# Wider products in a two-block transformer kernel: 512-column feed-forward products, 33-column slot factors, 512-column memory slabs

## The chip, the core and the metric

The kernel runs on one core of a Trainium2 chip. The metric is the device time of one execution in microseconds, lower is better. The engines are called as in the profile: PE (TensorE matmul), PEld (TensorE weight load, which overlaps PE), DVE (VectorE), ACT (ScalarE), POOL (GpSimd) and SP (SyncE, whose queue issues the loads).

## The reference, cut to what matters

256 tokens of width 1024 pass through two blocks in float32. The first block is an attention mixer and a mixture of 32 experts (each token goes to 2 of them), the second has two layers, each a mixer, a cross-attention into 256 memory tokens and a gated feed-forward with a causal convolution of width 3 over the tokens.

```python
# experts, after the choice of 2 of 32 per token (weight = group share * softmax of the two)
ys = (silu(xb @ w_g[e]) * (xb @ w_u[e])) @ w_d[e]
out = zeros(T, D).at[slot_tok].add(ys * slot_w)

def mem_attention(h, mem_n, w_q, w_kv, q_gain, k_gain, w_o):
    kv = (mem_n @ w_kv).reshape(B, M, 2, X_HEADS, X_HEAD_DIM)
    k, v = rmsnorm(kv[:, :, 0], k_gain), kv[:, :, 1]
    ...

def conv_ffn(h, w_up, w_conv, w_down):          # w_up 1024 x 5632, w_down 2816 x 1024
    u = causal_dwconv(h @ w_up, w_conv)
    gate, val = split(u, 2)
    return (silu(gate) * val) @ w_down
```

## The kernel before, in words

**Products.** Every large product is made of split numbers: a weight slab `w` (128 x 2048, 1 MB) is loaded by SP's queue, ACT copies it to the rounded `h` in two halves of 1024 columns, and DVE makes the remainder `l` = `w` - `h`, also in halves (`slab`, line 554). The activations are split in the same way into `xh` and `xl` (`parts`, `norm_parts`, `xtiles`, line 593). A product is then three matmuls, `h`·`xh`, `l`·`xh` and `h`·`xl` (`mm3`, line 575). `fm` (line 678) makes one PSUM bank of two 128-row halves by 256 tokens from 8 pieces of the depth, so 48 matmuls of 256 columns. `tm` with `by_token_products` and `by_token_wide` (lines 693 to 709) makes the transposed form, tokens by 256 or by 512 columns.

**Feed-forward** (`ffn`, line 1567). 22 pairs, each 128 gate and 128 value columns. Per pair: one `fm` (48 matmuls), a DVE product with the reciprocal root mean square that also evicts the bank (`fu<-fm,rbc`), four DVE convolution steps (`fc<-fu,partile,fc`), Silu on ACT, gate times value on DVE, and the split of the result into `fa`. After every second pair comes `down`, 24 to 48 matmuls of 512 or 256 columns (`dn`) that add to four banks which are held throughout. In the second layer these four banks first receive the residual `x`, transposed by 16 products with the identity (lines 1572 to 1576), and the epilogue copies them out, two by ACT and two by DVE.

**Experts** (`moe`, line 1061). Four gathers of 8 experts each (`gather`, line 1112): DVE makes a 0/1 selection `st` and two scaled copies of it, `rt` (times the token's norm factor `rtm`) and `ct` (times its weight); PE gathers the tokens (`ga`) and takes 8 one-column products of `rt` and `ct` (`rs`), which give each slot's norm and weight. Expert weights go straight from the load into the products (`gu<-w,xs`, `by`), without a split, and take any spare buffer. Steps of the memory part (`memory`, line 1335: per layer one `prepare`, four `values` of 256 columns by `by_token_products` and four `keys`) are filled in: `MEM_EARLY` ahead of the first gather, `MEM_EVERY` per group.

**Order.** The helper records every operation (all at line 471 of the profile), and `plan` (line 292) lays them out per engine by a list schedule with costs from `price`; loads stay in recorded order unless a due time moves them (`touch`, line 261 in the part on first uses, sets how a tile's first load is ranked). PSUM has 3 banks of tag `g` (`fm`, `tm`, `ga`), 2 of `a`, 2 of `b`, 1 of `m` (`bank`, line 486). `w`, `h` and `l` have 3 buffers each.

Of the kernel before, what the change touches and what calls it, by code (L numbers as in the profile page):

```python
# [25 lines left out]
NPAIR = 22  # L26
WARM = 44
# [6 lines left out]
MEM_EARLY = 2  # L34
FILL = 300
LATEG = 1
MEM_EVERY = (2, 2, 2, 2, 2, 2, 1, 0)
# [16 lines left out]
for _name, _width in (("ident", 128), ("cmask", 128), ("smask", 128), ("ulow", 128), ("ntri", 128),  # L54
                      ("bd64", 128), ("dist", 256), ("cm", 32), ("sm", 32), ("cb", 16), ("sb", 16),
                      ("slot", 32)):
    CST[_name] = (_off, _off + _width)
    _off += _width
# [104 lines left out]
class Recorder:  # L163
# [310 lines left out]
class Net:  # L474
# [118 lines left out]
    def xtiles(self):  # L593
        return [self.rec.tile([128, KC, T], F32R, n, n, 2) for n in ("xh", "xl")]
# [72 lines left out]
    def norm_parts(self, src, gain, stats=True):  # L667

        acc = None
        xh, xl = self.xtiles()  # L670
# [5 lines left out]
        return (xh, xl), acc  # L676

    def fm(self, w, x, kcs=None, cols=0, name="fm", tag="g"):

        (h, l), _ = w  # L680
        xh, xl = x
# [10 lines left out]

    def tm(self, b, w, x, kcs, t, cols, first=True, last=True):

        (h, l), _ = w
        xh, xl = x
# [275 lines left out]
    def route(self, rtm):  # L972
# [16 lines left out]
        def small(name, *s):  # L989
            if name in ("wt", "place", "wlate"):  # L990
                return self.small(name, 2, *s, bufs=1)
# [26 lines left out]
        sel, wt = small("sel", 4, 8), small("wt", 4, 8)  # L1018
# [3 lines left out]
        sel, wtf = (q.rearrange("p t g e -> p t (g e)") for q in (sel, wt))  # L1022
# [36 lines left out]
        return wtf, place, wlate, flag  # L1059

    def moe(self, steps, early, every):
        nc, a, x = self.rec, self.a, self.x

        hh, hl = (t.rearrange("p (t q) n -> p t (q n)", t=2) for t in self.xtiles())
# [9 lines left out]
        wt, place, wlate, flag = self.route(rtm)  # L1074
# [5 lines left out]
        xs, rest = self.gather(0, hh, hl, place, wt, rtm)  # L1080
        banks = [self.bank("a", "gu")]
        self.gate_up(0, range(KC), xs, banks[0])
        for g in range(8):
# [17 lines left out]
            if g % 2 == 0 and g < 6:  # L1101
                ahead, later = self.gather(g // 2 + 1, hh, hl, place, wt, rtm)
# [9 lines left out]
    def gather(self, p, hh, hl, place, wt, rtm):  # L1112
# [3 lines left out]
        ct, rt = (self.temp("b", n, [128, 2, 8, SLOTS]) for n in ("ct", "rt"))  # L1116
        for t in range(2):
# [3 lines left out]
            nc.vector.tensor_scalar(rt[:, t], st[:, t], rtm[:, t:t + 1], None, ALU.mult)  # L1121
            nc.vector.tensor_tensor(ct[:, t], st[:, t], pe(wt), ALU.mult)
        stv, ctv, rtv = (v.rearrange("p t e s -> p t (e s)") for v in (st, ct, rt))
        xs = self.big("xs", [128, KC, 256])
        for i in range(4):
# [6 lines left out]
            for j in range(2):  # L1132
# [4 lines left out]
                else:  # L1137
                    nc.vector.tensor_scalar(xs[:, c, :], b[:, 256 * j:256 * j + 256], gc, None, ALU.mult)
        b = self.bank("m", "rs")
# [6 lines left out]
        nc.vector.tensor_copy(rw, b[:, :4])  # L1146

        b = self.bank("m", "sb")
        for i in range(2):
            for t in range(2):  # L1150
                o = 256 * i + 128 * t
                nc.tensor.transpose(b[:, o:o + 128], stv[:, t, 128 * i:128 * i + 128].step("bitcast", F32), self.ident)
# [121 lines left out]
    def two_norms(self):  # L1274
# [7 lines left out]
        xh, xl = self.xtiles()  # L1282
# [52 lines left out]
    def memory(self):  # L1335
# [5 lines left out]
        def prepare(l):  # L1341
# [4 lines left out]
            xh, xl = self.xtiles()  # L1346
# [17 lines left out]
        def keys(l, s):  # L1364
            b = self.fm(self.slab(a[f"w_xkv{l}"][s], 256), state["x"], tag="b" if l and s > 1 else "g")
# [3 lines left out]
        def values(l, s):  # L1369
            bs = self.by_token_products(self.slab(a[f"w_xkv{l}"][4 + s], 256), state["x"])  # L1370
            for t in range(2):
                nc.scalar.activation(self.mem_v[l][:, t, 256 * s:256 * s + 256], bs[t][:, :256], AF.Copy,
# [3 lines left out]
        for l in range(2):  # L1376
            steps.append(lambda l=l: prepare(l))
            steps += [lambda l=l, s=s: values(l, s) for s in range(4)]
# [188 lines left out]
    def ffn(self, l, out=None):  # L1567
# [12 lines left out]
        def down(i):  # L1580
# [10 lines left out]
            else:  # L1591
                for t in range(2):
                    s = slice(128 * t, 128 * t + 128)
                    for n in range(2):
                        m = slice(512 * n, 512 * n + 512)
                        self.mm3([(acs[2 * t + n], part(0, k, s), part(1, k, s), h[:, k, m], lo[:, k, m], False,
                                   i == ndown - 1 and k == 1) for k in range(2)])

        for i in range(NPAIR):
            p = "ab"[i % 2]  # L1600
            b = self.fm(self.slab(a[f"w_up{l}"][i], 256), x)
# [46 lines left out]
def layouts(i):  # L1648
# [41 lines left out]
    for l in range(2):  # L1690
        o[f"w_xq{l}"] = slabs(f["x_w_q_2"][l], 8, 256)
        o[f"w_xkv{l}"] = slabs(f["x_w_kv_2"][l], 8, 256)
# [39 lines left out]
def shape_constants():  # L1732
# [15 lines left out]
    for cn, sn, half in (("cm", "sm", 16), ("cb", "sb", 8)):  # L1748
# [3 lines left out]
        for n, fn in ((cn, np.cos), (sn, np.sin)):  # L1752
            put(n, fn(ang.astype(np.float64)).reshape(2, 128, half).transpose(1, 0, 2))
    put("slot", np.broadcast_to(np.arange(SLOTS) - 999.0, (128, SLOTS)))
# [17 lines left out]
```

## Time and profile before

| | before |
|---|---|
| median of 3 runs (lowest to highest) | 1273.33 us (1271.55 to 1277.99) |
| profiled execution: its own time / span | 1273.8 / 1272.0 us |
| mean granted clock over the span | 0.982 of full speed |
| PE, DVE, ACT busy | 1219.8, 862.5, 647.9 us |
| DMA | 273.5 MB, mean 215 GB/s |

An execution's own time is 1.8 us more than its span. A chain piece is a stretch in which the named engine was the one that the end waited for. Names are out<-in with buffer numbers left out. Where PE runs back to back, the time of a matmul is the step from one to the next, since each one's listed duration overlaps its neighbours.

### The profile page before, as it was taken

Reading aid. Unit: us, or ns where it says so; the run is one execution under the profiler, and the core shown is the slowest. Engines: PE = TensorE matmul, PEld = TensorE weight load, DVE = VectorE, ACT = ScalarE, POOL = GpSimd, SP = SyncE. Lnnn points to the kernel's source line nnn. Section 1 sums busy time; section 2 is a strip of 40 time slices with the busy share of each in tenths; the row PEclk is TensorE's granted clock in tenths of the full one; section 3 lists DMA queues with packets and bytes.
Section 4 is the critical chain, followed back from the end, with each engine's and each line's share of the span. In section 5 each row is a group of like instructions: output and inputs, shape, how many; then the busy total and the mean of one; then the engine's idle time right before and its main releaser. Section 6 shows DMA issues by size and latency. Waiting matters only on the chain.

```text
span 1272.0 us, 22373 instructions
## 1 busy us (share of the span) xinstructions
PE 1219.8 (96%) x9175; PEld 1074.6 (84%) x9175; DVE 862.5 (68%) x1546; ACT 647.9 (51%) x1095; POOL 7.9 (1%) x70
## 2 busy tenths in 40 slices
PE   9999999997889978998999999999999999999998
PEld 9988999664555644897999999999989999999997
DVE  7667677424462345997777977777755587877775
ACT  7655554223332235554555655455767655555543
POOL 0000000000000000000000000000000000000000
PEclk9999999998899999998999999999999999999999
DMA  7633665899999997542541555454433252555551
GB/s 274 237 103 130 217 247 199 340 405 417 382 398 419 415 381 282 199 153 80 181 151 67 210 195 182 177 199 168 172 125 135 103 178 97 185 199 171 187 176 64
DMA packets 40140, 273.51 MB, mean 215 GB/s; under 512 B 4576, under 2 KB 4576, under 8 KB 8032
## 3 DMA queue, kind: packets, MB, share of 16 engines
q1 hardware_dynamic: 40032, 272.03, 57.5%
q8 instruction: 73, 1.20, 0.4%
q14 instruction: 35, 0.29, 0.1%
HBM read 270.96 MB, written 1.05 MB: 214 GB/s over the span
## 4 chain that ended last, share of the span: by engine, by line
PE 68%; DVE 5%; ACT 3%; issue 1%; DVEq 0%; ACTq 0%
PE fm L471 41%; PE dn L471 10%; PE tw L471 3%; PE gu L471 2%; PE tm L471 2%; PE oz L471 2%; DVE l L471 1%; PE mo L471 1%; PE by L471 1%; PE ms L471 1%; PE hn L471 1%; PE bo L471 1%; ACT h L471 1%; DVE x L471 1%; PE co L471 1%
## 5 line engine op out<-in xcount | busy, mean ns | idle before, releaser
L471 PE MATMUL fm<-xh,h 128*128 128x256 f32 x1824 | 527.3, 290 | 5.1 <-ACT h L471 2.9
L471 PE MATMUL fm<-xh,l 128*128 128x256 f32 x1824 | 519.8, 285 | 6.2 <-DVE l L471 6.2
L471 PE MATMUL fm<-xl,h 128*128 128x256 f32 x1824 | 519.5, 285 | 0.0
L471 DVE TENSOR_TENSOR l<-w,h 128x1024 fp32r<-128x1024 f32 (+2 forms) x328 | 383.6, 1192 | 60.8 <-ACT h L471 59.3
L471 ACT ACTIVATE h<-w 128x1024 fp32r<-128x1024 f32 (+2 forms) x328 | 325.9, 1028 | 170.7 <-issue 87.3
L471 PEld LDWEIGHTS fm<-xh,h 128*128 128x128 f32 x1824 | 351.4, 193 | 16.6 <-ACT h L471 5.8
L471 PEld LDWEIGHTS fm<-xh,l 128*128 128x128 f32 x1824 | 351.6, 193 | 9.0 <-DVE l L471 8.6
L471 PEld LDWEIGHTS fm<-xl,h 128*128 128x128 f32 x1824 | 351.7, 193 | 6.5 <-issue 5.1
L471 DVE SCALAR_TENSOR_TENSOR fc<-fu,partile,fc 128x256 f32<-128x256 f32 x176 | 73.5, 480 | 1.3 <-ACT fc L471 1.3
L471 PE MATMUL gu<-w,xs 128*32 128x512 f32 x512 | 68.7, 644 | 0.1
L471 PE MATMUL dn<-fa,h 128*128 128x256 f32 x352 | 64.2, 282 | 1.1 <-ACT fa L471 0.6
L471 PE MATMUL tm<-l,xh 128*128 128x256 f32 (+2 forms) x204 | 59.9, 294 | 2.7 <-DVE l L471 2.7
L471 PE MATMUL tm<-h,xh 128*128 128x256 f32 (+2 forms) x204 | 61.1, 300 | 0.8 <-DVE x L471 0.6
L471 PE MATMUL tm<-h,xl 128*128 128x256 f32 (+2 forms) x204 | 59.7, 294 | 0.0
L471 PE MATMUL dn<-h,fa 128*128 128x512 f32 x176 | 57.0, 396 | 0.0
L471 DVE TENSOR_TENSOR fu<-fm,rbc 128x512 f32<-128x512 f32 x44 | 30.3, 688 | 37.9 <-PE fm L471 37.6
L471 PEld LDWEIGHTS dn<-fa,h 128*128 128x128 f32 x352 | 54.4, 189 | 1.6 <-ACT fa L471 0.8
L471 DVE SCALAR_TENSOR_TENSOR yl<-by,rw,yh 128x512 fp32r<-128x512 f32 x16 | 12.0, 749 | 55.7 <-ACT yh L471 55.7
L471 PE MATMUL dn<-fa,l 128*128 128x256 f32 x176 | 49.6, 282 | 0.0
L471 ACT ACTIVATE fc<-fc 128x256 f32<-128x256 f32 x44 | 18.4, 419 | 56.2 <-DVE fc L471 56.2
L471 PEld LDWEIGHTS tm<-h,xh 128*128 128x128 f32 x204 | 39.7, 195 | 5.4 <-issue 2.5
L471 PEld LDWEIGHTS tm<-l,xh 128*128 128x128 f32 x204 | 39.9, 196 | 3.5 <-DVE l L471 3.1
(285 smaller groups left out, 1545.5 us busy)
## 6 DMA issues: line engine op xcount, KB each, us to landing
w<-w_gu SPq DMA_DIRECT2D x64, 1024.0 KB, 10.8
w<-w_up SPq DMA_DIRECT2D x44, 1024.0 KB, 4.9
w<-w_dn SPq DMA_DIRECT2D x32, 1024.0 KB, 12.2
w<-w_down SPq DMA_DIRECT2D x22, 1024.0 KB, 4.9
w<-w_xkv SPq DMA_DIRECT2D x16, 1024.0 KB, 8.8
w<-w_in_d SPq DMA_DIRECT2D x8, 1024.0 KB, 4.9
w<-w_xq SPq DMA_DIRECT2D x8, 1024.0 KB, 4.9
w<-w_xo SPq DMA_DIRECT2D x8, 1024.0 KB, 4.9
```

The costliest lines, as they stand in the source:

```text
L471: self.last[engine.engine] = getattr(engine, method)(*map(r, a), **{n: r(v) for n, v in k.items()})
```

## The change

1. **Feed-forward in 512 columns.** For pairs 3 to 19 of the 22, in both layers, `fm_wide` takes the place of `fm`. The tile `xx` now holds `xh` and `xl` side by side, so per half and piece of the depth one matmul `h`·[`xh`|`xl`] of 512 columns and one `l`·`xh` of 256 stand where three of 256 stood. Each half has a bank of its own, whose two column halves must be added: ACT copies the first 256 columns to `fu`, DVE adds the second 256, and then the product with `rbc` runs from SBUF.
2. **Second layer's residual.** The 16 identity products at the start are gone; at pair 5, 16 transposes go through the one `m` bank into `xt` (4 ACT copies), and the epilogue is four DVE additions.
3. **Gather.** `rt` and `ct` are gone. `rs` is four products per gather of the selection with `factors` (33 columns: norm factor and 32 weights), followed by a copy, a mask product with the constant `own` and a short reduction.
4. **Memory values.** Two half-input slabs of 512 columns per step by `by_token_wide`, two steps per layer instead of four; `MEM_EARLY` 1, `MEM_EVERY` (1,2,2,2,1,1,1,0).
5. **One tile for both activation parts**, and in the rank of a tile's first use the time that the planner allows a load to land (`lag`) is now taken off too.

```diff
-            op.preds.setdefault(t.first.idx, -t.first.cost)
+            op.preds.setdefault(t.first.idx, -t.first.cost - t.first.lag)
...
     def xtiles(self):
-        return [self.rec.tile([128, KC, T], F32R, n, n, 2) for n in ("xh", "xl")]
+        both = self.rec.tile([128, 2, KC, T], F32R, "xx", "xx", 2)
+        return both[:, 0], both[:, 1], both
...
+    def fm_wide(self, w, x):
+        (h, l), _ = w
+        xh, _, both = x
+        bs = []
+        for j in range(2):
+            b = self.bank("g", "fw")
+            s = slice(128 * j, 128 * j + 128)
+            for k in range(KC):
+                self.rec.record("tensor", [
+                    ("matmul", (b[:, :512].rearrange("p (a b) -> p a b", a=2), h[:, k, s], both[:, :, k, :]),
+                     dict(start=k == 0, stop=False, skip_group_check=True)),
+                    ("matmul", (b[:, :T], l[:, k, s], xh[:, k, :]),
+                     dict(start=False, stop=k == KC - 1, skip_group_check=True))])
+            bs.append(b)
+        return bs
...
-            nc.vector.tensor_scalar(rt[:, t], st[:, t], rtm[:, t:t + 1], None, ALU.mult)
-            nc.vector.tensor_tensor(ct[:, t], st[:, t], pe(wt), ALU.mult)
...
-        for n, v in enumerate((rtv, ctv)):
-            for i in range(2):
-                for t in range(2):
-                    self.mm(b[:, 2 * n + i:2 * n + i + 1], v[:, t, 128 * i:128 * i + 128], self.kone,
-                            t == 0, t == 1)
+        for i in range(2):
+            for t in range(2):
+                self.mm(b[:, 64 * i:64 * i + 33], one(t, i), factors[:, t, :], t == 0, t == 1)
...
         def values(l, s):
-            bs = self.by_token_products(self.slab(a[f"w_xkv{l}"][4 + s], 256), state["x"])
+            bs = self.by_token_wide([self.slab(w, 512) for w in a[f"w_xv{l}"][2 * s:2 * s + 2]], state["x"])
...
-        if out is not None:
-            for c in range(KC):
-                for t in range(2):
-                    self.mm(acs[2 * t + c // 4][:, 128 * (c % 4):128 * (c % 4) + 128],
-                            self.x[:, c, 128 * t:128 * t + 128], self.ident, c % 4 == 0, False)
...
-            nc.vector.tensor_tensor(u[:, :, 2:], self.two(b), self.rep(rbc), ALU.mult)
+            if NARROW <= i < NPAIR - 2:
+                for n, b in enumerate(self.fm_wide(slab, x)):
+                    nc.scalar.activation(u[:, n, 2:], b[:, :T], AF.Copy)
+                    nc.vector.tensor_tensor(u[:, n, 2:], u[:, n, 2:], b[:, T:], ALU.add)
+                nc.vector.tensor_tensor(u[:, :, 2:], u[:, :, 2:], self.rep(rbc), ALU.mult)
...
+            if i == 5 and out is not None:
+                xt = self.big("xt", [128, 2, D])
+                for t in range(2):
+                    for n in range(2):
+                        b = self.bank("m", "xt")
+                        for j in range(4):
+                            nc.tensor.transpose(b[:, 128 * j:128 * j + 128],
+                                                self.x[:, 4 * n + j, 128 * t:128 * t + 128], self.ident)
+                        nc.scalar.activation(xt[:, t, 512 * n:512 * n + 512], b, AF.Copy)
...
-                if i % 2:
-                    nc.vector.tensor_copy(o, acs[i])
-                else:
-                    nc.scalar.activation(o, acs[i], AF.Copy)
+                nc.vector.tensor_tensor(o, acs[i], xt[:, t, 512 * n:512 * n + 512], ALU.add)
```

**How it moves the instructions.** First DVE in the first layer's feed-forward, pairs 10 and 11 (`fu` the up-projection, `fc` its convolution, `fa` the split result, `l` the slabs' remainders); before:

```order
L471 TENSOR_TENSOR fu<-fm,rbc 128x2x256
L471 TENSOR_TENSOR l<-w,h 128x1024
L471 SCALAR_TENSOR_TENSOR fc<-fu,partile,fc 128x256 x4
L471 TENSOR_TENSOR l<-w,h 128x1024
L471 TENSOR_TENSOR fc<-fc 128x256
L471 TENSOR_TENSOR fa<-fc,fa 128x256
L471 TENSOR_TENSOR fu<-fm,rbc 128x2x256
```

After, the same pairs, from the addition for pair 10's second half:

```order
L472 TENSOR_TENSOR fu<-fu,fw 128x256
L472 TENSOR_TENSOR l<-w,h 128x1024
L472 TENSOR_TENSOR fu<-fu,rbc 128x2x256
L472 TENSOR_TENSOR fu<-fu,fw 128x256
L472 SCALAR_TENSOR_TENSOR fc<-fu,partile,fc 128x256 x4
L472 TENSOR_TENSOR l<-w,h 128x1024
L472 TENSOR_TENSOR fu<-fu,fw 128x256
L472 TENSOR_TENSOR fc<-fc 128x256
L472 TENSOR_TENSOR fu<-fu,rbc 128x2x256
```

The addition for pair 11's first half now stands ahead of pair 10's convolution, so the convolution is behind a wait for PE's next half.

Next PE at the first gather (`ga` the gathered tokens, `gu` the first expert group); before:

```order
L471 MATMUL ga<-st,xl 128x256
L471 MATMUL rs<-order,rt 128x1 x4
L471 MATMUL rs<-order,ct 128x1 x4
L471 MATMUL gu<-w,xs 32x512 x4
L471 MATMUL sb<-csttile,st 128x128 x4
```

After:

```order
L472 MATMUL ga<-st,xx 128x256 x2
L472 MATMUL rs<-factors,st 128x33
L472 MATMUL ga<-st,xx 128x256 x28
L472 MATMUL rs<-factors,st 128x33 x3
L472 MATMUL gu<-w,xs 32x512 x4
L472 MATMUL sb<-csttile,st 128x128 x4
```

Half as many `rs` products stand between the gather and the first expert product, and no `ct` or `rt` is waited for.

Last, SP at the head of the program (three slabs of `w_in_a` in quarters, and the quarters of `x`); before:

```order
2 L471 DMA x_87<-x 128x512
3 L471 DMA w_100<-w_in_a 128x512
4 L471 DMA w_113<-w_in_a 128x512
5 L471 DMA w_126<-w_in_a 128x512
6 L471 DMA x_87<-x 128x512
7 L471 DMA w_100<-w_in_a 128x512
8 L471 DMA x_87<-x 128x512
```

After:

```order
2 L472 DMA x_87<-x 128x512
3 L472 DMA w_100<-w_in_a 128x512
4 L472 DMA x_87<-x 128x512
5 L472 DMA w_100<-w_in_a 128x512
6 L472 DMA x_87<-x 128x512
7 L472 DMA w_100<-w_in_a 128x512
8 L472 DMA x_87<-x 128x512
9 L472 DMA w_100<-w_in_a 128x512
10 L472 DMA w_153<-w_in_a 128x512 x4
11 L472 DMA w_168<-w_in_a 128x512 x4
```

The first quarters of the second and third slab have moved from ahead of the second quarter of `x` to behind the whole of `x` and the first slab.

## Rows read from the trace of the kernel before

**Rows 1.** The page: busy time of each engine, and the chain's shares by engine and line.

```profile
PE 1219.8 (96%) x9175; PEld 1074.6 (84%) x9175; DVE 862.5 (68%) x1546; ACT 647.9 (51%) x1095; POOL 7.9 (1%) x70
...
PE 68%; DVE 5%; ACT 3%; issue 1%; DVEq 0%; ACTq 0%
PE fm L471 41%; PE dn L471 10%; PE tw L471 3%; PE gu L471 2%; PE tm L471 2%; PE oz L471 2%; DVE l L471 1%; PE mo L471 1%; PE by L471 1%; PE ms L471 1%; PE hn L471 1%; PE bo L471 1%; ACT h L471 1%; DVE x L471 1%; PE co L471 1%
```

**Rows 2.** The chain's pieces in order of time: start, length, engine, product, instructions.

```profile
514.47 7.04 PE tw L471 x31
...
729.06 11.52 PE fm L471 x96
740.57 5.76 PE dn L471 x48
...
1075.82 3.57 PE dn L471 x32
...
1108.47 11.51 PE fm L471 x96
1119.98 5.61 PE dn L471 x24
```

**Rows 3.** Stretch, length, then busy: two feed-forwards, experts; last granted clock, DMA share, GB/s.

```profile
729.06:867.24 138.18, 138.18 (x1154) 138.18 (x1154) 105.25 (x161) 73.24 (x113) 1.35 (x13) 1.00 0.53 185
1108.47:1245.43 136.96, 136.96 (x963) 128.19 (x962) 105.37 (x161) 73.09 (x113) 1.34 (x13) 1.00 0.53 184
225.00:500.00 275.00, 236.60 (x1738) 147.57 (x1737) 113.02 (x211) 86.02 (x126) 0.00 (x0) 0.94 0.98 398
```

**Rows 4.** DVE's longest wait between 1108 and 1245 us: total, times, longest.

```profile
DVE fu L471 <- PE fm L471: 16.1, 8, 2.1
```

**Rows 5.** Groups of instructions with shapes kept apart: busy, mean ns of one, idle before.

```profile
L471 DVE TENSOR_TENSOR l<-w,h 128x1024 fp32r<-128x1024 f32 x306 | 367.3, 1222 | 55.4 <-ACT h L471 53.9
...
L471 DVE SCALAR_TENSOR_TENSOR fc<-fu,partile,fc 128x256 f32<-128x256 f32 x176 | 73.5, 480 | 1.3 <-ACT fc L471 1.3
...
L471 DVE TENSOR_TENSOR xl<-bo,xh 128x256 fp32r<-128x256 f32 x16 | 6.7, 420 | 8.8 <-ACT xh L471 8.8
L471 ACT ACTIVATE xh<-bo 128x256 fp32r<-128x256 f32 x16 | 6.1, 383 | 10.0 <-PE bo L471 9.9
...
L471 DVE TENSOR_TENSOR ct<-st,wt 128x256 f32<-128x256 f32 x8 | 3.3, 418 | 0.0
```

**Rows 6.** PE in order of time, end of the first attention and start of the experts.

```profile
210.73 1.03 PE L471 MATMUL xt<-csttile,x 128*128 128x128 f32 x8
211.70 0.62 PE L471 MATMUL rt<-x,wr 128*36 128x256 f32 x2
...
233.17 0.95 PE L471 MATMUL rs<-order,rt 128*128 128x1 f32 x8
233.98 1.03 PE L471 MATMUL rs<-order,ct 128*128 128x1 f32 x8
234.94 1.07 PE L471 MATMUL gu<-w,xs 128*32 128x512 f32 x8
```

**Rows 7.** What SP's queue waited for between 225 and 500 us.

```profile
SPq L471 <- PE gu L471: 88.0, 45, 8.1
SPq L471 <- DVE l L471: 62.9, 10, 8.9
```

**Rows 8.** PE, then DVE, at the head, in order of time.

```profile
5.56 0.39 PE L471 MATMUL fm<-xh,h 128*128 128x256 f32 x1
...
25.00 0.28 PE L471 MATMUL fm<-xh,l 128*128 128x256 f32 x1
...
9.16 0.87 DVE L471 SCALAR_TENSOR_TENSOR xl<-x,partile,xh 128x256 fp32r<-128x256 f32 x2
10.02 0.69 DVE L471 TENSOR_TENSOR l<-w,h 128x512 fp32r<-128x512 f32 x1
10.63 0.69 DVE L471 TENSOR_TENSOR acc<-acc,sq 128x512 f32<-128x512 f32 x1
```

More of the change, by code (lines that the diff above doesn't have):

```diff
@@ L669, in norm_parts @@
         acc = None
-        xh, xl = self.xtiles()
+        xh, xl, both = self.xtiles()
         for i in range(4):
@@ L1058, in route @@
         nc.vector.tensor_copy(flag[0:1, :], b[0:1, 0:1])
-        return wtf, place, wlate, flag
+        return factors, place, wlate, flag
     def moe(self, steps, early, every):
         nc, a, x = self.rec, self.a, self.x
-        hh, hl = (t.rearrange("p (t q) n -> p t (q n)", t=2) for t in self.xtiles())
+        hh, hl = (t.rearrange("p (t q) n -> p t (q n)", t=2) for t in self.xtiles()[:2])
         for q in range(2):
@@ L1073, in moe @@
         rtm = self.rstd_by_token(self.sumsq(x))
-        wt, place, wlate, flag = self.route(rtm)
+        factors, place, wlate, flag = self.route(rtm)
         nc.bias = -FILL
@@ L1079, in moe @@
         self.next = []
-        xs, rest = self.gather(0, hh, hl, place, wt, rtm)
+        xs, rest = self.gather(0, hh, hl, place, factors)
         banks = [self.bank("a", "gu")]
@@ L1101, in moe @@
             if g % 2 == 0 and g < 6:
-                ahead, later = self.gather(g // 2 + 1, hh, hl, place, wt, rtm)
+                ahead, later = self.gather(g // 2 + 1, hh, hl, place, factors)
             if q:
@@ L1110, in moe, with gather @@
                 steps.pop(0)()
-    def gather(self, p, hh, hl, place, wt, rtm):
+    def gather(self, p, hh, hl, place, factors):
         nc, slot = self.rec, self.c("slot")
         st = self.temp("a", "st", [128, 2, 8, SLOTS], F32R)
-        ct, rt = (self.temp("b", n, [128, 2, 8, SLOTS]) for n in ("ct", "rt"))
         for t in range(2):
@@ L1138, in gather @@
                     nc.vector.tensor_scalar(xs[:, c, :], b[:, 256 * j:256 * j + 256], gc, None, ALU.mult)
+        one = lambda t, i: stv[:, t, 128 * i:128 * i + 128].step("bitcast", F32)
         b = self.bank("m", "rs")
-        for n, v in enumerate((rtv, ctv)):
-            for i in range(2):
-                for t in range(2):
-                    self.mm(b[:, 2 * n + i:2 * n + i + 1], v[:, t, 128 * i:128 * i + 128], self.kone,
-                            t == 0, t == 1)
-        rw = self.small("rw", 4)
-        nc.vector.tensor_copy(rw, b[:, :4])
+        for i in range(2):
+            for t in range(2):
+                self.mm(b[:, 64 * i:64 * i + 33], one(t, i), factors[:, t, :], t == 0, t == 1)
+        bv = b[:, :128].rearrange("p (i n) -> p i n", i=2)
+        rw = self.small("rw", 4)
+        own = self.small("own", 2, 8, bufs=1)
+        nc.vector.tensor_copy(rw[:, 0:2], bv[:, :, 0])
+        nc.vector.tensor_tensor(own, bv[:, :, 1 + 8 * p:9 + 8 * p],
+                                self.c("own").rearrange("p (i e) -> p i e", i=2), ALU.mult)
+        nc.vector.tensor_reduce(rw[:, 2:4], own, axis=AX.X, op=ALU.add)
         b = self.bank("m", "sb")
@@ L1151, in gather @@
                 o = 256 * i + 128 * t
-                nc.tensor.transpose(b[:, o:o + 128], stv[:, t, 128 * i:128 * i + 128].step("bitcast", F32), self.ident)
+                nc.tensor.transpose(b[:, o:o + 128], one(t, i), self.ident)
         sb = self.small("sb", 2, T, dt=F32R)
@@ L1364, in keys @@
         def keys(l, s):
-            b = self.fm(self.slab(a[f"w_xkv{l}"][s], 256), state["x"], tag="b" if l and s > 1 else "g")
+            b = self.fm(self.slab(a[f"w_xk{l}"][s], 256), state["x"], tag="b" if l and s > 1 else "g")
             self.head_norm("ab"[s % 2], b, self.k256, True, state["r"], self.mem_k[l][:, s],
@@ L1377, in memory @@
             steps.append(lambda l=l: prepare(l))
-            steps += [lambda l=l, s=s: values(l, s) for s in range(4)]
+            steps += [lambda l=l, s=s: values(l, s) for s in range(2)]
             steps += [lambda l=l, s=s: keys(l, s) for s in range(4)]
@@ L1595, in down @@
                         m = slice(512 * n, 512 * n + 512)
-                        self.mm3([(acs[2 * t + n], part(0, k, s), part(1, k, s), h[:, k, m], lo[:, k, m], False,
-                                   i == ndown - 1 and k == 1) for k in range(2)])
+                        self.mm3([(acs[2 * t + n], part(0, k, s), part(1, k, s), h[:, k, m], lo[:, k, m],
+                                   i == 0 and k == 0, i == ndown - 1 and k == 1) for k in range(2)])
         for i in range(NPAIR):
             p = "ab"[i % 2]
-            b = self.fm(self.slab(a[f"w_up{l}"][i], 256), x)
+            slab = self.slab(a[f"w_up{l}"][i], 256)
             u = self.temp(p, "fu", [128, 2, T + 2])
             nc.gpsimd.memset(u[:, :, 0:2], 0.0)
-            nc.vector.tensor_tensor(u[:, :, 2:], self.two(b), self.rep(rbc), ALU.mult)
+            if NARROW <= i < NPAIR - 2:
[3 more added lines that the diff above has]
+                nc.vector.tensor_tensor(u[:, :, 2:], u[:, :, 2:], self.rep(rbc), ALU.mult)
+            else:
+                nc.vector.tensor_tensor(u[:, :, 2:], self.two(self.fm(slab, x)), self.rep(rbc), ALU.mult)
             cs = self.temp(p, "fc", [128, 2, T])
@@ L1691, in layouts @@
         o[f"w_xq{l}"] = slabs(f["x_w_q_2"][l], 8, 256)
-        o[f"w_xkv{l}"] = slabs(f["x_w_kv_2"][l], 8, 256)
+        o[f"w_xk{l}"] = slabs(f["x_w_kv_2"][l][:, :1024], 8, 256)
+        o[f"w_xv{l}"] = halves(f["x_w_kv_2"][l][:, 1024:])
         o[f"w_xo{l}"] = slabs(f["x_w_out_2"][l], 8, 256)
@@ L1753, in shape_constants @@
             put(n, fn(ang.astype(np.float64)).reshape(2, 128, half).transpose(1, 0, 2))
+    put("own", np.arange(8)[None, None, :] == 4 * np.arange(2)[None, :, None] + r[:, :, None] // 32)
     put("slot", np.broadcast_to(np.arange(SLOTS) - 999.0, (128, SLOTS)))
```

32 lines of the change are left out of this document (19 added, 13 removed).

## The prediction, made before the changed kernel was run

> **What bounds the kernel now.** I read the busy totals first, then the chain of waits, then the stretches. PE is busy for 1219.8 of 1272.0 us, and the chain goes through PE for 68% of the span, through DVE for 5% and ACT for 3%; 41% of the span is the feed-forward's up-projection alone [rows 1]. So what shortens PE's stream in the feed-forwards shortens the kernel, as long as nothing else ends later. The chain's pieces give the pace: 96 matmuls of 256 columns in 11.52 us, 0.120 us each; 31 matmuls of 512 columns in 7.04 us, 0.227 each; in the down-projection of layer 1, 24 of 512 columns in 5.61 us, 0.234 each [rows 2]. In both feed-forwards PE fills eight rounds (two pairs and one down-projection each) without a gap, 136.96 us or 17.12 per round in layer 1, while DVE works 105.37 and ACT 73.09 [rows 3]: DVE has 13.17 us of work per round and idles 3.95, ACT has 9.14. DVE's largest wait there is for PE's finished bank [rows 4]. The experts are another regime: between 225 and 500 us PE is busy for 236.60 of 275 us, but the DMA engines for 98% of it, at 398 GB/s [rows 3], and SP's queue waits for `gu` products to give buffers back, 88.0 us in 45 waits [rows 7]. There transfers set the end, and PE time saved is worth nothing until the transfers end earlier.
>
> The sum stands against the profiled execution's own 1273.8 us, 0.5 us above the median of 1273.33. A measurement of this kernel can tell about 0.5%, 6.4 us: faster is below 1266.96, slower above 1279.7.
>
> **Term 1, the merged products.** 17 pairs in 2 layers, 8 pieces of the depth and 2 halves make 544 places where two matmuls of 256 columns become one of 512. Two cost 0.240. The one costs 0.2271 by the memory rows or 0.2338 by the down-projection [rows 2], the nearest rows there are; both multiply the same number format with a weight load per matmul. Saved: 544 × 0.0129 = 7.0 or 544 × 0.0062 = 3.4 us. I take the middle, 0.2305, since the down-projection shares the stage and the memory rows the form: **−5.2**.
>
> **Term 2, layer 1's opening.** The identity products go: 32 instructions, 3.57 us [rows 2]. The 16 transposes that come instead step at 0.121 us by the eight that took from 210.73 to 211.70 [rows 6]: 1.94 us. Net −1.6. They use the only `m` bank in four groups, so each group may wait for ACT to empty it (up to 1.65 us, an estimate: a 512-column ACT copy behind one 1.05 us half of `h`); products of the next pair stand between the groups and cover most of that. Bounds −1.6 and 0; I take **−1.1**.
>
> **Term 3, the first gather.** Here PE waits for no transfer: `rs` takes from 233.17 to 234.94, 1.77 us for 16 instructions [rows 6]. Half of them remain, 33 columns instead of one: −0.9. The memory steps filled in ahead of the gather change from 96 matmuls of 256 columns (11.5 us) to 48 of 512 (11.06): −0.45. Together **−1.35**. The scaled copies (`ct` takes 0.418 us each [rows 5], `rt` less) lay behind those fillers, so their removal adds nothing on the path; the tiny mask and sum stand beside the `sb` transposes.
>
> **Term 4, the other experts.** The bytes are the same: 16 memory slabs, eight of them in another form. Two slabs must now be there before a `values` step ends, and both hold a `w` buffer, which queues SP's next expert loads behind DVE's `l` (already 62.9 us in 10 waits [rows 7]); against that, two steps fewer per layer and no `rt`/`ct` let buffers go sooner. The transfers leave 2% of 275 us open, 5.5 us [rows 3]; that is the most that tighter queueing could give back, and I put as much on the other side. I take **0**, bounds −5 and +5.
>
> **Term 5, the head.** Loads of the second and third slab move behind `x`. Before, the first 144 products took from 5.56 to 25.12 us [rows 8], 2.3 more than 144 × 0.12. After, in the first four quarters only one slab is there: 12 products, 1.44 us per quarter, against DVE's 0.87 + 0.69 + 0.69 = 2.25 [rows 8] for the quarter of `xl`, `l` and the squares. Three such gaps of 0.81 are 2.4. With the queue of three more loads behind, **+0.4**; bounds −1 and +1.5.
>
> **Term 6, the new evictions.** Per round four ACT copies of 256 columns from PSUM (0.383 each by `xh<-bo`) and four DVE additions (0.420 each by `xl<-bo,xh`) are added [rows 5]; the `rbc` product stays. DVE: 13.17 + 1.68 = 14.85; ACT: 9.14 + 1.53 = 10.7. PE's new round is 2 × 16 × (0.2305 + 0.120) + 5.6 = 16.8. Both fit, so **0**; what hides them is PE, and the cover on DVE is 2.0 us per round where it was 3.95. With three `g` banks a half's bank is wanted again two halves later, 5.6 us; its drain is an ACT copy and an addition, behind at most one `l` half of 1.22 and four convolution steps of 0.48 each [rows 5]: 0.38 + 1.22 + 1.92 + 0.42, some 4 us. If that cover went, each round would be late by what is missing, times 17. The end gains nothing: the four additions replace copies behind the same last products.
>
> The sum: −5.2 − 1.1 − 1.35 + 0 + 0.4 + 0 = −7.25, so **1266.5 us**.
>
> **Rivals.** *The wide product gains nothing (chance 0.13).* If the pace goes by columns, a merged product costs as much as its two parts and term 1 is 0: 1273.8 − 1.1 − 1.35 + 0.4 = 1271.8. For it: the two 512-column rows differ by 0.007, half of the saving, and the one of this very stage is the dearer. Against it: even that one saves 0.006. The Trainium skill ("TensorE: Matmul & The Clock Gate", section Back-to-back issue gap) gives an isolated gap of N/2.4 + 2.5 ns, by which one product in place of two saves only 2.5 ns, 544 × 2.5 = 1.4 us, an estimate, and the kernel would come out at 1270.4. The trace speaks against it: 0.120 at 256 columns, where that rule has 0.109, leaves 13 ns per instruction over the columns.
>
> *DVE becomes the feed-forward's bound (chance 0.13, slower).* The place is DVE's queue in the rounds: the addition for the next pair's first half now stands ahead of this pair's convolution, so the convolution, Silu, `fa` and the down-projection behind them wait for PE's next half. It decides as soon as DVE's waits per round exceed the 2.0 us left. Today they are 3.95, nearly all for PE or ACT. If three quarters remain, 2.96, the round is 14.85 + 2.96 = 17.8, 0.7 more than 17.12; 17 rounds add 11 us in place of term 1: 1273.8 + 11 − 2.05 = 1282.8. Against it: waits for PE shrink by themselves when DVE is fuller, since work that waits for nothing (six halves of `l`) fills them. The Trainium skill ("Perfetto Trace Analysis", section Identifying Performance Opportunities) reads the same gap repeated on the saturated engine as a sign of too few buffers; three banks for twice as many evictions would be such a place, and PE showed no such gap in these rounds before.
>
> *The experts' transfers lose (chance 0.13):* term 4 at +5, 1271.5. For it: two slabs hold buffers at once; against it: SP's queue already runs ahead until it waits for a buffer. *They gain (chance 0.16):* term 4 at −5, 1261.5.
>
> **How the numbers follow.** The forecast has the remaining chance, 0.45. Its own range by the bounds of terms 1 to 3 and 5 is 1262.9 (−7.0 − 1.6 − 1.35 − 1) to 1270.6 (−3.4 − 1.35 + 1.5); 0.25 of it lies below 1266.96 and 0.20 above. With the gaining transfers (0.16) faster has 0.41; the first and third rival with 0.20 give 0.46 for no change; the DVE rival gives 0.13 for slower. The range goes from 1258.5 (term 4 at −5 and term 1 at its better bound give 1259.8, and the head may gain) to 1276 (the transfers' loss with the worse bounds of terms 1, 2 and 5: 1275.6); outside are the DVE rival and a small rest.
>
> **What would show it.** Term 1: the wide matmuls step at 0.227 to 0.234 and a round takes 16.8 us with no PE gap. Term 2: no `dn` piece before the first `fm` of layer 1, and at most short gaps among the transposes. Term 3: the first `gu` starts about 1.35 us earlier, near 233.6. Term 4: the stretch from the first to the last expert product keeps its length and its DMA share. Term 5: 144 head products end near 25.5. The prediction is wrong if PE shows gaps behind `fa` or a `g` bank in the rounds (DVE's bound), or if the experts' stretch changes by more than 5 us.

## The result and the profile after

The changed kernel takes 1262.17 us (median of 5 runs, 1260.68 to 1265.47) against 1273.33: a ratio of 0.9901 with a 95% interval from 0.9875 to 0.9927. That is faster by 11.2 us, more than the 6.4 that the prediction set as its bound. The forecast was 1266.5, and 1258.5 to 1276 its range; faster had the chance 0.41 there and no change 0.46. The profiled execution took 1262.97 us; the page says:

```profile
span 1261.2 us, 20928 instructions
...
PE 1208.7 (96%) x8391; PEld 1026.1 (81%) x8391; DVE 878.7 (70%) x1609; ACT 671.4 (53%) x1157; POOL 7.6 (1%) x70
...
PE 66%; DVE 4%; DMA 3%; ACT 2%; issue 1%; ACTq 0%; DVEq 0%
PE fm L472 26%; PE fw L472 15%; PE dn L472 10%; PE tw L472 4%; DMA w<-w_dn 3%; PE gu L472 2%; PE oz L472 2%; PE mo L472 1%; PE ms L472 1%; PE by L472 1%; DVE l L472 1%; PE hn L472 1%; PE bo L472 1%; PE co L472 1%; ACT h L472 1%; DVE rsq_t L472 1%
```

Against [rows 1], PE lost 11.1 us of work and still bounds the kernel; DVE gained 16.2 and ACT 23.5 us. DMA now has a share of the chain, most of it two loads of an expert's weights (`w_dn`) for which the end waited: the experts' part is told below.

I cut both traces at the same places of the program and compared the lengths of the pieces, each from the first instruction of one product to that of the next one named:

| piece of the program | before | after | difference |
|---|---|---|---|
| start to the transposed norm `bt` | 25.21 | 25.86 | +0.65 |
| `bt` to the first expert product `gu` | 209.73 | 208.64 | -1.09 |
| experts: first `gu` to the 31 `tw` after them | 279.18 | 278.75 | -0.43 |
| even mixer, to the last `mo` of layer 0 | 169.43 | 168.29 | -1.14 |
| feed-forward of layer 0, to the first `oz` | 225.89 | 221.45 | -4.44 |
| odd mixer and cross-attention, to the last `mo` | 150.10 | 150.19 | +0.09 |
| feed-forward of layer 1 and output | 212.46 | 207.97 | -4.49 |
| span | 1272.00 | 1261.15 | -10.85 |

Each column is one execution. The experts' piece scatters most: in the five kernels below that have the changed kernel's experts (experiments 1, 2, 4, 7 and 8) it takes 276.35 to 278.74 us, so its -0.43 could as well be -2.8.

**The feed-forwards.** The chain's pieces (start, length, engine, product, instructions) show the rounds that answer to [rows 2]:

```profile
726.87 11.09 PE fw L472 x64
737.97 5.70 PE dn L472 x48
743.66 11.11 PE fw L472 x64
754.77 5.64 PE dn L472 x48
...
1092.81 5.60 PE dn L472 x24
1098.42 11.10 PE fw L472 x64
...
1133.81 11.30 PE fw L472 x64
1145.11 5.60 PE dn L472 x24
```

Two pairs take 11.10 us where they took 11.52: 32 merged products and 32 single ones, 0.347 per couple. With 0.120 for the single one, the 512-column product costs 0.227, the better of the two bounds. PE has no gap, and the stretch that answers to the first in [rows 3] (columns as there) says how far DVE and ACT were from the bound:

```profile
720.00:860.85 140.85, 140.85 (x953) 130.04 (x953) 120.27 (x204) 88.65 (x152) 1.44 (x14) 1.00 0.55 190
```

Per round of 16.74 us DVE works 14.3 (120.27 / 140.85 × 16.74) and ACT 10.5; the prediction had 14.85 and 10.7.

**Layer 1's opening.** PE, in order of time, at the transposes that took the place of the identity products (start, duration):

```profile
1114.95 0.60 PE L472 MATMUL xt<-csttile,x 128*128 128x128 f32 x4
1115.30 0.48 PE L472 MATMUL fw<-xx,h 128*128 128x512 f32 x1
...
1116.80 0.66 PE L472 MATMUL xt<-csttile,x 128*128 128x128 f32 x4
1117.21 0.47 PE L472 MATMUL fw<-xx,h 128*128 128x512 f32 x1
```

Each group of four takes 0.35 to 0.41 us, and eight products run until the next group; no group waits for ACT to empty the one bank.

**The experts' first products.** What answers to [rows 6]:

```profile
233.82 0.75 PE L472 MATMUL rs<-factors,st 128*128 128x33 f32 x6
234.50 1.07 PE L472 MATMUL gu<-w,xs 128*32 128x512 f32 x8
```

The `rs` products between the gather and the first expert product shrank from 1.77 to 0.68 us. The start of `gu` itself moved only from 234.94 to 234.50, since the head came later.

**One difference that is not the change's.** The even mixer's 1.14 us lie after a stretch in which PE had little to do. The program is the same there, but TensorE came back from the lower to the higher of its two clock levels at another moment. From both traces, the stretch after PE's restart; the third number from the end is the granted clock. Before (restart at 590.36):

```profile
592.00:596.00 4.00, 4.00 (x22) 4.00 (x21) 2.10 (x8) 0.42 (x1) 0.00 (x0) 0.53 0.00 0
```

After (restart at 589.30):

```profile
590.00:594.00 4.00, 4.00 (x26) 4.00 (x26) 3.01 (x10) 1.01 (x5) 0.00 (x0) 0.68 0.01 2
```

The kernels of experiments 9 and 11 run the same instructions in the same order up to the end of this piece, and it takes 169.51 and 168.53 us in them. So such a microsecond comes and goes without an edit, and it belongs to no term.

### The profile page after: what moved, and what is told of

It reads as the page before. It is cut to its first block, busy times and chain, and to the rows that moved or that the text cites. A ratio compares the mean times of both kernels' runs of the same rounds, so it can differ in the third digit from the quotient of the medians.

```text
span 1261.2 us, 20928 instructions
## 1 busy us (share of the span) xinstructions
PE 1208.7 (96%) x8391; PEld 1026.1 (81%) x8391; DVE 878.7 (70%) x1609; ACT 671.4 (53%) x1157; POOL 7.6 (1%) x70
## 4 chain that ended last, share of the span: by engine, by line
PE 66%; DVE 4%; DMA 3%; ACT 2%; issue 1%; ACTq 0%; DVEq 0%
PE fm L472 26%; PE fw L472 15%; PE dn L472 10%; PE tw L472 4%; DMA w<-w_dn 3%; PE gu L472 2%; PE oz L472 2%; PE mo L472 1%; PE ms L472 1%; PE by L472 1%; DVE l L472 1%; PE hn L472 1%; PE bo L472 1%; PE co L472 1%; ACT h L472 1%; DVE rsq_t L472 1%
## 5 line engine op out<-in xcount | busy, mean ns | idle before, releaser
L472 PE MATMUL fm<-xx,h 128*128 128x256 f32 x2560 | 485.4, 290 | 5.2 <-DVE cu L472 2.2
L472 PEld LDWEIGHTS fm<-xx,h 128*128 128x128 f32 x2560 | 406.5, 194 | 20.2 <-issue 11.9
L472 PE MATMUL fm<-xx,l 128*128 128x256 f32 x1280 | 367.3, 287 | 8.5 <-DVE l L472 8.4
L472 PEld LDWEIGHTS fm<-xx,l 128*128 128x128 f32 x1280 | 247.8, 194 | 12.7 <-DVE l L472 10.7
L472 PE MATMUL fw<-xx,h 128*128 128x512 f32 x544 | 190.8, 394 | 0.0
L472 PE MATMUL fw<-xx,l 128*128 128x256 f32 x544 | 152.3, 280 | 0.0
L472 PEld LDWEIGHTS fw<-xx,h 128*128 128x128 f32 x544 | 101.9, 187 | 22.7
L472 PEld LDWEIGHTS fw<-xx,l 128*128 128x128 f32 x544 | 102.7, 189 | 0.3
L472 PE MATMUL tw<-h,xx 128*128 128x512 f32 x288 | 95.9, 399 | 0.2 <-DVE x L472 0.2
L472 PE MATMUL tw<-l,xx 128*128 128x512 f32 x144 | 57.2, 397 | 2.1 <-DVE l L472 2.1
```

What stands on the lines that cost most here:

```text
L472: self.last[engine.engine] = getattr(engine, method)(*map(r, a), **{n: r(v) for n, v in k.items()})
```

## The experiments

All kernels ran beside the kernel before on the same chip; ratios are to it. Pieces are those of the table, from one execution each.

**1. The products split again.** Two matmuls of 256 columns for each of 512, everything else as in the changed kernel.

```diff
-("matmul", (b[:, :512]..., h[:, k, s], both[:, :, k, :]), ...),
+("matmul", (b[:, :T], h[:, k, s], both[:, 0, k, :]), ...),
+("matmul", (b[:, T:], h[:, k, s], both[:, 1, k, :]), ...),
```

> The changed kernel with each 512-column product of the feed-forward written as two of 256 again; banks per half, copies and additions stay. Theory (a matmul costs its columns plus some 13 ns, so merging is what saves): 32 merged pairs of matmuls, 11.10 to 11.30 us now, go back to 11.5 per two pairs, a round to about 17.2 in both layers, and the time to about 1262.2 + 7 = 1269. Rival (the saving comes from the bank per half and the shorter eviction, not from merging): rounds stay at 16.7 to 16.8 and the time within 1.5 of 1262.

Measured: 1268.83 us, ratio 0.9958 (0.9943 to 0.9973), 6.7 above the changed kernel by the medians. Its chain in layer 0:

```profile
726.40 11.51 PE fw L472 x96
737.91 5.63 PE dn L472 x48
```

The up-projection is back at 11.51, so merging is what saves: 0.41 us per 32 merges, 13 ns each in these rounds. The two feed-forward pieces take 224.71 and 210.54 us, 5.83 more than in the changed kernel, which is 10.7 ns for each of the 544 merges. The down-projection of layer 0 stays at 5.63 where it was 5.76 [rows 2]; that small gain is not the merging's.

**2. The old ranking of loads.**

```diff
-op.preds.setdefault(t.first.idx, -t.first.cost - t.first.lag)
+op.preds.setdefault(t.first.idx, -t.first.cost)
```

> The changed kernel with the old ranking of first uses (no lag), so the first quarters of the second and third slab load ahead of the second quarter of x again. Theory (the head's new load order lost 0.65 us): first product near 5.6, the 48 products after the head's norm start 0.65 earlier (25.4 against 26.07) and the time is 1261.5. Rival (the rank also sets the order of later loads, above all among the experts): the head is the same or better, and the experts' stretch changes by more than 1 us in either direction.

Measured: 1261.33 us, ratio 0.9909 (0.9876 to 0.9943). `bt` came at 24.67 us against 25.86, but over all profiles of this study it lies between 24.67 and 27.80 with the old ranking and between 25.61 and 27.05 with the new one, medians 25.7 and 25.9. The head's 0.65 us are within what the first loads scatter, and this run does not settle the term.

**3. Memory values in 256 columns again,** with `MEM_EARLY` 2 and the old steps.

```diff
-bs = self.by_token_wide([self.slab(w, 512) for w in a[f"w_xv{l}"][2 * s:2 * s + 2]], state["x"])
+bs = self.by_token_products(self.slab(a[f"w_xv{l}"][s], 256), state["x"])
```

> The changed kernel with memory values in slabs of 256 columns, four steps per layer, filled in as before (2 early, then 2,2,2,2,2,2,1,0); the gather and the feed-forward stay changed. Theory (the two-slab step holds the loads up: between 355 and 375 us the DMA moved 311 and 198 GB/s, some 6 us lost, while the new gather saves elsewhere): that hole goes, the experts' stretch from the first expert product to the 31 products at 513 us shrinks from 278.75 to about 274, the time to about 1258. Rival one (bytes set the stretch, holes only move): 278 to 280 and 1262 to 1263. Rival two (the wide values saved in other places what the hole cost): 283 or more and 1266.

Measured: 1258.49 us, ratio 0.9872 (0.984 to 0.9904), and the experts' piece of the table takes 273.09 us instead of 278.75. The changed kernel lost it in one place. Two stretches of its trace (columns as in [rows 3], the last two are the DMA share and GB/s):

```profile
355.00:365.00 10.00, 9.20 (x68) 4.56 (x67) 6.63 (x16) 6.57 (x13) 0.00 (x0) 1.00 0.80 311
365.00:375.00 10.00, 8.73 (x58) 2.68 (x56) 3.02 (x6) 0.73 (x2) 0.00 (x0) 0.83 0.58 198
```

SP's queue, in order of time, shows why: behind 358.21 nothing is issued until both slabs of layer 1's first values find buffers at 370.07.

```profile
358.21 0.99 SPq L472 DMA_DIRECT2D w<-w_dn  x2
370.07 1.59 SPq L472 DMA_DIRECT2D w<-w_xv  x2
```

With single slabs the queue waits there too, but only until 359.78, and the same stretches read:

```profile
355.00:365.00 10.00, 8.57 (x67) 3.76 (x66) 7.46 (x17) 6.57 (x13) 0.00 (x0) 1.00 0.96 388
365.00:375.00 10.00, 8.43 (x65) 3.51 (x65) 3.56 (x7) 3.05 (x4) 0.00 (x0) 1.00 1.02 425
```

So the experts' part was 6.1 us shorter than before once the slabs were as before: something else in the change gives 6 us there. The kernels of experiments 5, 9 and 11 run the same experts' code as this one and take 272.64, 272.55 and 271.78 us.

**4. The old opening of layer 1's feed-forward,** identity products and copies.

```diff
+if out is not None:
+    for c in range(KC):
+        for t in range(2):
+            self.mm(acs[2 * t + c // 4][:, ...], self.x[:, c, 128 * t:128 * t + 128], self.ident, c % 4 == 0, False)
...
-if i == 5 and out is not None:
...
```

> The changed kernel with the 16 identity products ahead of the second feed-forward of layer 1 and the old epilogue of copies. Theory (PE's stream there is the bound, and the 16 transposes cost 1.8 us where the products cost 3.57): 1.8 us more, 1264. Rival (the products ran while PE would have waited for the norm anyway, so nothing is gained by moving them): the first product of the up-projection starts no later than now relative to the mixer's end, and the time stays at 1262.

Measured: 1263.13 us, ratio 0.9913 (0.9883 to 0.9942), too near to tell by the time alone. The trace tells it: from the last `mo` to the end 209.72 us against 207.97, 1.75 more.

**5. The new gather alone** in the kernel before; it also has the one tile for both activation parts, which the new code brings. Of the change's diff only the parts on `gather`, `route` (`factors`), `own` and `xtiles` stay:

```diff
-for n, v in enumerate((rtv, ctv)):
...
+self.mm(b[:, 64 * i:64 * i + 33], one(t, i), factors[:, t, :], t == 0, t == 1)
```

> The kernel before with the new gather alone (33-column products, no scaled copies): no wide products in the feed-forward, 256-column memory slabs, old opening and epilogue, old ranking of loads. With 256-column slabs the experts' stretch took 273.1 us, against 279.2 before, so something in the gather must have given 6. Theory (the scaled copies and the products that waited for them held the loads: SP's queue waited 6.5 us for one copy before): first expert product 0.9 earlier, the stretch behind it about 273 to 274, the time 1273.5 - 0.9 - 5.5 = 1267. Rival (the order that the planner chose for the other changed parts gave it, and the gather gives only its own products): the stretch stays at 278 to 280 and the time is 1272.5.

Measured: 1266.07 us, ratio 0.9935 (0.9912 to 0.9959), and 272.64 us for the experts' piece. The gather gives 6.5 us in this piece, and the traces show where. PE at the second gather, before (in brackets the idle time and its releaser):

```profile
246.49 1.90 PE L471 MATMUL by<-w,act 128*32 128x512 f32 x16
250.34 0.35 PE L471 MATMUL rs<-order,rt 128*128 128x1 f32 x2 [1.94 <-DVE rt L471]
...
252.03 1.84 PE L471 MATMUL rs<-order,ct 128*128 128x1 f32 x8
...
254.10 0.63 PE L471 MATMUL co<-sb,yh 128*128 128x256 f32 x2
```

And with the new gather:

```profile
246.19 1.90 PE L472 MATMUL by<-w,act 128*32 128x512 f32 x16
248.02 1.08 PE L472 MATMUL rs<-factors,st 128*128 128x33 f32 x8
...
250.51 0.40 PE L472 MATMUL co<-sb,yh 128*128 128x256 f32 x2
```

Before, PE stood for 1.94 us behind a scaled copy that DVE had not made yet, and then TensorE ran at its lower level (what brought it is not shown; see experiment 6): the granted clock was 0.80 of full from 245 to 255 us against 1.00, and the 16 `rs` products took 3.4 us where the first gather's took 1.77. The first expert output `co` came 19.2 us after the first `gu` instead of 15.9. The rest was lost at the last gather: between the 65th and the 81st `co` matmul before took 37.3 us and this kernel 33.9. PE waited for no scaled copy there; 14 of the 16 `rs` products stood in one block ahead of `sb`:

```profile
406.40 0.83 PE L471 MATMUL rs<-order,rt 128*128 128x1 f32 x6
407.10 1.03 PE L471 MATMUL rs<-order,ct 128*128 128x1 f32 x8
```

Each expert product that comes late gives its buffer back late [rows 7], and the loads queue behind it: the `w_dn` pair after the second gather is issued at 265.54 us before and at 261.46 here. The down-projections of layer 0 take 5.63 us in this kernel too, so their small gain is neither the merging's nor the wide slabs'. The one tile `xx` is what the feed-forward here shares with experiment 1, but no run has that tile alone, so the cause is open.

**6. The same with the scaled copies made, but read by nobody.**

```diff
+nc.vector.tensor_scalar(rt[:, t], st[:, t], factors[:, t, 0:1], None, ALU.mult)
+nc.vector.tensor_tensor(ct[:, t], st[:, t], pe(factors[:, :, 1:33]), ALU.mult)
```

> The gather_only kernel with the two scaled copies of the selection made again on DVE in every gather, but read by nobody. Theory (what held the experts was PE, which stood in order behind products that waited for the copies): with no product behind them the copies cost next to nothing, the first expert output (co) comes 15.9 us after the first expert product as without them, the stretch stays at 272.6 to 274, the time at 1266 to 1267. Rival (DVE's time and the two buffers they take cost it, or their place in DVE's order): co comes at 18 to 19 us, the stretch is 276 to 279 and the time 1270 to 1272.

Measured: 1269.78 us, ratio 0.9964 (0.9949 to 0.9979), between the two. Its profiled execution was 8.8 us above its median, so I took one more.

> The same kernel with unread scaled copies once more, for a profile near its median of 1269.8 (the profiled execution of the first was 8.8 us above it). It is 3.7 above the kernel without the copies, half of what the whole gather gave. Theory one (the wait in PE's order at the second gather was worth the first 3.2 us, and copies anywhere in DVE's queue cost the rest later): first expert output at 15.4 to 15.9 us after the first expert product, and the 3 to 4 us are lost at a later gather, behind the copies in DVE's queue. Theory two (the planner's order with the copies differs elsewhere): the loss stands at a place with no copy near it.

Measured: 1269.83 us. The first `co` comes 15.4 us after the first `gu`, so it was PE's products behind the copies that cost 3 us up to there. The ninth is 1.6 us later than in experiment 5, but there TensorE ran at its lower level again, this time without a wait for a copy:

```profile
245.00:255.00 10.00, 8.35 (x58) 4.61 (x57) 6.82 (x15) 2.58 (x3) 0.00 (x0) 0.85 1.01 425
```

That delay is gone by the 33rd `co`, where this kernel is 0.1 us ahead of experiment 5. By the 81st it is 1.9 late, where the kernel before is 6.5 late. Another 2.7 us are lost between the 89th and 97th, with no copy near. It takes 25.5 us for these eight steps and experiment 5 takes 22.9. But experiments 3 and 11, which run the same experts' code as experiment 5 and make no copy, take 25.5 too, so that loss says nothing of the copies or of the planner's order.

What this leaves: the medians put the unread copies at 3.7 of the gather's gain. The kernel lies 4.1 below the kernel before, of which 2.3 are outside the experts (0.8 ahead of the first expert product, 1.5 in the feed-forwards), so some 2 us, an estimate, are left to the products that read the copies. How the 3.7 divide between the copies' time on DVE, their buffers and the order that the planner chose stays open.

**7. One more copy on DVE.** The evictions' first halves go to DVE instead of ACT.

```diff
-nc.scalar.activation(u[:, n, 2:], b[:, :T], AF.Copy)
+nc.vector.tensor_copy(u[:, n, 2:], b[:, :T])
```

> The changed kernel with the copy of the first column half of each feed-forward bank on DVE instead of ACT: four copies of 0.42 us per round move, so that DVE has 14.3 + 1.7 = 16.0 us of work in a round of 16.74. Theory (PE's stream sets the round as long as DVE's own work fits): rounds stay at 16.74 to 16.8 and the time within 1 of 1262. Rival (DVE's waits need more than the 0.7 left, as my slower case had it): rounds of 17 or more with PE idle ahead of the wide products or of the down-projection, 17 rounds by 0.3 or more, 1267 or more.

Measured: 1261.0 us, one run. The stretch of layer 0's rounds:

```profile
718.40:859.00 140.60, 140.60 (x952) 129.86 (x952) 131.30 (x236) 77.08 (x118) 1.43 (x14) 1.00 0.56 190
```

PE has no gap although DVE now works 15.6 of each 16.74 us. DVE's waits shrink with its free time, as the argument against the slower rival said, and leave PE alone.

**8. All 22 pairs wide.**

```diff
-if NARROW <= i < NPAIR - 2:
+if 0 <= i < NPAIR:
```

> The changed kernel with all 22 pairs per layer in 512 columns instead of 17. Theory (each merged product saves 13 ns): 5 pairs x 2 layers x 16 x 13 ns = 2.1 us less, 1260. Rival (at the edges PE waits for DVE: the first pairs come while the norm and its parts are still made, and after the last pair the longer eviction stands ahead of the last down-projection): gaps at the edges of a few tenths to 1 us each, and the time is 1262 or more.

Measured: 1263.18 us, ratio 0.9908 (0.9885 to 0.993). Layer 1 gained 1.03 us (206.94 from the last `mo` to the end), just the 80 merges; layer 0 lost 1.8, at its last down-projection:

```profile
881.34 0.86 PE L472 MATMUL dn<-fa,h 128*128 128x256 f32 x5 [2.85 <-ACT fa L472]
```

In the changed kernel two waits stand there, 0.67 and 0.55, so 1.6 less in all. After the last pair no other product covers the longer eviction. Part of the loss is the clock's: behind this wait it was granted at 0.83 of full, where the changed kernel had 1.00 in the same stretch:

```profile
880.00:890.00 10.00, 8.66 (x60) 8.66 (x61) 6.94 (x15) 6.73 (x14) 0.00 (x0) 0.83 0.33 115
```

**9. The three together:** 256-column slabs, old ranking, all wide; the edits of 2, 3 and 8 in one kernel.

> Everything that looked good together: the changed kernel with 256-column memory slabs as before, the old ranking of loads, and all 22 pairs wide. Theory (the gains are in different stages and add): 1258.5 - 0.9 - 2.1 = 1255.5, below both kernels. Rival (all-wide costs at the edges): 1257.6 or more.

Measured: 1258.82 us, ratio 0.9876 (0.9856 to 0.9897): the wide edges cost again what the rest gave. The wait ahead of layer 0's last down-projection is 2.85 us here too, the clock behind it 0.66 from 875 to 885 us, and layer 0's feed-forward takes 224.41 us where experiment 8 took 223.27.

**10. The two-slab steps moved** by one expert group.

```diff
-MEM_EVERY = (1, 2, 2, 2, 1, 1, 1, 0)
+MEM_EVERY = (1, 2, 2, 1, 2, 1, 1, 0)
```

> The changed kernel with MEM_EVERY (1,2,2,1,2,1,1,0) in place of (1,2,2,2,1,1,1,0), which puts the second layer's memory norm one expert group later, with its first two-slab step behind it. Theory (two slabs that must both find buffers behind the memory norm stop SP's queue wherever this happens): the hole in the DMA rate goes from 355 to 375 us to some 35 us later, and the time stays at 1261 to 1263. Rival (it was that one place, where an expert group's buffers came late): the DMA runs at over 400 GB/s throughout, the experts' stretch is 273 to 275 and the time 1258.

Measured: 1258.99 us, ratio 0.9889 (0.9873 to 0.9904), the experts' piece 273.36 us. The stretch that moved 198 GB/s reads

```profile
365.00:375.00 10.00, 8.65 (x72) 3.33 (x74) 3.95 (x7) 1.16 (x2) 0.00 (x0) 1.00 1.01 422
```

and up to 425 us no stretch of 10 us moves less than 400 GB/s. My theory that two-slab steps stop the queue wherever they stand falls: it was that step in that place, where two buffers at once were not to be had before `gu` products had run behind the memory norm (SP's longest wait there, 10.8 us, is for a `gu`).

**11. The best that these point to:** 256-column slabs, old ranking, pairs 0 to 19 of layer 0 and all of layer 1; the edits of 2 and 3, and

```diff
-if NARROW <= i < NPAIR - 2:
+if i < (NPAIR if l else NPAIR - 2):
```

> The changed kernel with 256-column memory slabs and their old steps, the old ranking of loads, pairs 0 to 19 of layer 0 and all 22 of layer 1 wide. In the all-wide kernel layer 1 gained 1.1 us and layer 0 lost 1.8 ahead of its last down-projection (PE idle for 2.85 us there against 0.67). Theory (only the last two pairs of layer 0 lose): 1258.5 - 0.9 (head) - 1.1 - 0.6 = 1256. Rival (the first pairs are no gain in layer 0, since the norm stands there): 1256.6 to 1257.5.

Measured: 1256.03 us (median of 5, 1254.86 to 1262.61), ratio 0.9874 (0.9852 to 0.9897), the lowest median here, some 6 us below the changed kernel. Its lead over experiment 3 is within the intervals, and the two ratios are alike (0.9874 and 0.9872).

## Why the prediction came out as it did

- **Term 1, merging: right, mis-sized.** Forecast −5.2 with bounds −7.0 and −3.4. The traces give −5.9 (the two feed-forward pieces of the table without term 2 and the 1.3 of layer 0's down-projections), and experiment 1 takes back 5.8 by the traces, 6.7 by the medians. The product itself costs the better bound, 0.227. The row that carried over is the one at 514 us, which the prediction calls the memory's; it belongs to the even mixer's values (`w_ev`). The down-projection's 0.234 did not carry over. That the whole −7.0 is not reached is seen in layer 1, where every second round's pairs take 11.30 us instead of 11.10; why, no run tells.
- **Its rival, no gain: wrong.** The Trainium skill ("TensorE: Matmul & The Clock Gate", Back-to-back issue gap) gives 2.5 ns over the columns for an isolated product, and says itself that in a stream of weight loads and products the spacing goes by both. Experiment 1 measured 11 to 13 ns per merge, so the isolated figure does not hold for this stream.
- **Term 2, the opening: right, mis-sized.** Forecast −1.1, measured −1.75 (experiment 4): the 0.5 for waits at the one `m` bank was not spent.
- **Term 3, the first gather: right.** Forecast −1.35, measured −1.09 from `bt` to `gu`. Experiment 5, with the new gather alone, has −0.82 there where −0.9 was forecast; the wide memory step gives −0.28 (208.64 against the 208.92 of experiment 3) instead of −0.45.
- **Term 4, the other experts: the size right by accident, the working wrong.** Forecast 0, measured −0.43, but as −6.1 and +5.7 (experiments 3 and 5). Term 3 said that the scaled copies' "removal adds nothing on the path"; that was read at the first gather, where fillers hide them, and it fails at the second, where PE waited 1.94 us for one and then ran at the lower clock. The trace before had that row. The most that quicker buffers could give was put at 5.5 us, 2% of the stretch at 398 GB/s; the gather alone gave 6.5, and single stretches run at 422 to 425 GB/s (experiments 3 and 10), so the room was larger. And the two-slab step lost about as much at one place, near the price that the third rival had; it and the fourth both happened, in one run, and cancelled. That the forecast came so near is luck in this term: with the gain alone the time is 1258.49 (experiment 3), at the lower end of the range.
- **Term 5, the head: open.** Forecast +0.4, read as +0.65, within the scatter of the first loads. The three gaps that its working had are there, but the steps show 0.3 to 0.5 us instead of 0.81; and the first product is late, at 6.51 us against 5.56.
- **Term 6 and the slower rival: right and wrong.** The evictions cost nothing in the rounds, and experiment 7 shows that DVE could take more. (The rival's own price was added wrongly: 17 rounds of 0.69 us are 11.7, not 11.) At the last pairs, which the change left narrow, they do cost (experiment 8). The Trainium skill ("Perfetto Trace Analysis", Identifying Performance Opportunities) takes repeated gaps on the saturated engine as a sign of too few buffers; with twice the evictions on three banks, PE shows none in the rounds, so no run here shows that case.

The sum of the terms, −7.25, missed 3.6 us against the profiled execution: 0.7 in term 1, 0.6 in term 2, 0.4 in term 4, 1.1 that the clock gave in the even mixer, and 1.3 in layer 0's down-projections, which no term had; the head and the gather take 0.5 back.

## What to carry to other kernels

Where PE's stream is the bound, two 256-column products with one weight tile are worth merging, at 11 to 13 ns for each merge in this kernel, as long as the longer eviction stands under other products: at the end of a chain it cost 1.8 us net, in part through the lower clock behind the wait. Where transfers are the bound, ask of the small PE products in between what they wait for and what stands behind them: 16 tiny products behind a late copy put the first expert output 3 us back, and 3.4 us more were lost at a later gather where they waited for no copy. Read a small difference from several executions: the same experts' code takes 276.35 to 278.75 us in six of them. And a term that comes out as nothing may be two that cancel; undoing one part alone shows it.

## What was not expected of the hardware

- In the kernel before, a PE wait of 1.94 us at the second gather is followed by the lower clock (0.80 over 10 us), and 16 products take 3.4 us instead of 1.77. Experiment 6 has the lower clock at the same place (0.85) without that wait, so the wait is not shown to be the cause.
- After one and the same wait of 2.85 us the clock is 0.83 in experiment 8 and 0.66 in experiment 9, over 10 us each, and the feed-forward of layer 0 takes 1.1 us more in the second.
- The 48 products of layer 0's down-projection take 5.76 us before and 5.63 to 5.70 in the kernels that lay the two activation tiles into one, though they read neither; the cause is open.
- The same kernel reached `bt` at 27.80 and at 25.48 us (experiment 6), so no edit at the head can be judged by one profile.
